# A hybrid decoder layer on one core: stored sums loaded behind the weights, and the order of sums at the seam of the MLP's matrices

## The chip, the cores and the metric

The kernel runs on one core of a Trainium2 chip. The time is the device time of one execution in microseconds (us). TensorE (PE) multiplies matrices, VectorE (DVE) and ScalarE (ACT) work on elements, GpSimd (POOL) and SyncE (SP) here mostly start transfers; the engines run side by side and wait for one another by semaphores.

## The reference, cut to what matters

512 rows of 2048 columns go through one layer: a norm, an input projection, a short gated convolution beside an attention, a merge through an output matrix with the residual, and then the MLP, where the change lies:

```
h = rmsnorm(x, g_mlp)
u = square(relu(einsum('bsd,df->bsf', h, w_ff1)))     # 2048 -> 8192
x = x + einsum('bsf,fd->bsd', u, w_ff2)               # 8192 -> 2048
return rmsnorm(x, g_final)
```

All of it is float32.

## The kernel before

Each large product is done with Strassen-Winograd's scheme: one level, seven products of half-size blocks in place of eight, named A11, A12, S4, S2, S3, S1, A22 after their left or right operands. The operands of S1 to S4 are sums of blocks. Each float32 operand is split into a high part of a type that TensorE takes (`th`, made by ACT in `high_of`, L111) and a low part, the rest (`tl`, made by DVE in `low_of`, L114); three multiplications (high by high, high by low, low by high) then make one product. So behind every weight block of 1 MB stand one ACT pass, one DVE pass and, for the S products, a DVE subtraction (`sub`, L128), and PE takes the high part first and the low part last. `th` and `tl` have two buffers each.

**First matrix.** `w_ff1` goes through in 16 groups of 512 columns (`Group`, `ff1`). From group 1 on a group is `head` (A11, A12) and `tail` (S4, S2, S3, S1, A22), with weights loaded by SP into four slots `x0` to `x3`. `put_u` scales and rectifies each quarter of the result, and `sums` squares it, forms the seven operands that the second matrix will want (a tile `r` of 7 blocks, by four short DVE operations in a row), splits them (ACT L1480 into `rh`, DVE L1481 back into `r`) and writes both to memory (`s_d`, L1483 and L1484, on POOL's queue). Sums that needn't be done at once are put off in the list `later` and done in the next group's `tail`, behind the copy `s2` of the accumulator `a` (`snap`, ACT L268) and ahead of product S3. That copy is also what frees bank `a` for product S1.

**Second matrix.** `w_ff2` goes through in 8 segments of 1024 rows, each in two units (`unit`) of 1024 columns, in the order A11, A12, S2, S3, S1, A22, S4. Its left operands are the stored sums: `load_sums` brings them in four pieces: piece 0 (A11, A12), piece 1 (S2, S3), piece 2 (S1, A22), piece 3 (S4), into tiles `us` that share their memory with operands of the first matrix. The weights `y00, y10, y01, y11` come by SP's queue into the same four slots, each as soon as its slot is free.

**The seam** is the first unit. Piece 0 is loaded on POOL's queue in the last group of `w_ff1`, piece 1 on POOL's queue behind that group, pieces 2 and 3 on SP's queue behind the first unit's weights. The first unit's subtractions are `y00 <- y01 - y00`, `t <- y11 - y00` (operand of S2), `y01 <- y11 - y01` (S3), `t <- y10 - t` (A22).

What sets the order: within one engine the framework places independent instructions by its own estimate of when they are ready, beginning from the order in the code; an instruction held by `keep_in_program_order` stays where the code has it, and `issue_after` puts what follows behind a given instruction. On the chip each engine takes its instructions strictly in the order given.

Of the kernel before, what the change touches and what calls it, by code (L numbers as in the profile page):

```python
# [8 lines left out]
F32 = mybir.dt.float32  # L9
# [36 lines left out]
def tile_hybrid_block(ctx: ExitStack, tc, x, g_mix, w_in, b_f, b_gate, conv_w, w_conv_out,  # L46
                      w_attn_out, w_mix_out, g_mlp, w_ff1, w_ff2, g_final, out):
    nc = tc.nc
    x, out = x[0], out[0]
# [35 lines left out]
    s_d = [dram.tile([P, 2, 4, 7, HS], F32, name=f"s_d{i}") for i in range(DFF // 1024)]  # L85
# [24 lines left out]
    def high_of(src, hi):  # L110
        return tied(nc.scalar.activation(out=hi, in_=src, func=AF.Copy))  # L111

    def low_of(src, hi, lo):
        return tied(nc.vector.tensor_tensor(out=lo, in0=src, in1=hi.bitcast(F32), op=ALU.subtract))  # L114

    def split(src, hi, lo):
        return high_of(src, hi), low_of(src, hi, lo)
# [9 lines left out]
    def sub(out, a, b):  # L127
        return nc.vector.tensor_tensor(out=out, in0=a, in1=b, op=ALU.subtract)  # L128

    def add(out, a, b):  # L130
        return nc.vector.tensor_tensor(out=out, in0=a, in1=b, op=ALU.add)
# [81 lines left out]
    free, later = [0, 1, 2, 3], []  # L213

    class Group:
# [3 lines left out]
        def __init__(self, view, c1, c2, w, ST, mm, banks, put, scale=1.0, extra={}, after=None, shift=SHIFT):  # L219
            self.extra, self.after, self.shift = extra, {} if after is None else after, shift  # L220
            self.view, self.cs, self.w, self.ST, self.mm, self.banks = view, (c1, c2), w, ST, mm, banks
            self.put, self.scale, self.at = put, scale, {}
            self.begun, self.queue, self.X = False, nc.sync, {}
            self.pinned, self.mid, self.apart, self.ready = False, {}, False, {}
            self.freed, self.summed, self.paced, self.half = lambda: None, False, False, {}
            self.nq = view.shape[0] // (2 * P)

        def load(self, i, j):
# [105 lines left out]
        def tail(self):  # L334

            X = self.quarters((0, 1), (1, 1))
            a = self.a
            c = self.acc("c")
            self.run(c, "S4", X[1, 1], True)
            sub(X[0, 0], X[0, 1], X[0, 0])  # L340
            sub(X[0, 1], X[1, 1], X[0, 1])
            sub(X[1, 1], X[1, 1], X[0, 0])
            self.run(a, "S2", X[1, 1], False)
            sub(X[1, 0], X[1, 0], X[1, 1])
            self.done(1, 1)
            s2 = self.snap(a)
            while later:
                later.pop(0)()
            d = self.acc("d")
            self.run(d, "S3", X[0, 1], True)  # L350
            self.done(0, 1)
            d1 = self.snap(d, self.scale)
            self.run(a, "S1", X[0, 0], False)
            self.done(0, 0)
            s4 = self.snap(a, self.scale)
            add(d1, d1, s4)
            self.put(1, 1, d1)
            self.plus(s4, c, self.scale)
            self.put(0, 1, s4)
            self.run(d, "A22", X[1, 0], False)  # L360
            self.done(1, 0)
            self.plus(s2, d)
            self.put(1, 0, s2)
# [384 lines left out]
    a, b = (gV0.acc(k)[0] for k in "ab")  # L748
# [771 lines left out]
    for g in range(4):  # L1520
# [24 lines left out]
        group = groups[g]  # L1545
# [55 lines left out]
    def load_sums(seg, ks, ST, queue=nc.gpsimd):  # L1601

        for k in ks:
            place, names = US[k]
            t = main.tile([P, 2, 4, len(names), HS], F32R, tag=f"t{place}", name="us")
            for e in range(2):
                queue.dma_start(out=t[:, e].bitcast(F32), in_=s_d[seg][:, e, :, 2 * k:2 * k + len(names)])
            for e, n in enumerate(names):
                ST[n] = moving(t[:, :, :, e])

    for g in range(1, DFF // S):
        group = ff1(g, ((2 + 2 * (g % 2),), (3,), (1 if g < DFF // S - 1 else 2,), (7,)))
        group.head(True, order=((0, 0), (0, 1), (1, 0)))
        if g == DFF // S - 1:
            us0 = {}
            load_sums(0, (0,), us0)
        group.tail()

    load_sums(0, (1,), us0)
    later.pop()()  # L1620
    ph.close()
    pp.close()
# [70 lines left out]
    def unit(seg, cg, ST):  # L1693

        a, d = banks2(cg, "a"), banks2(1 - cg, "d")
        if seg == 0:
            kept[cg] = banks2(2 + cg, "b")
        b = kept[cg]  # L1700
        X, at = {}, {}
        end = seg == NSEG - 1 and cg == 1
        for i, j in ((0, 1), (1, 1), (0, 0), (1, 0)) if end else ((0, 0), (1, 0), (0, 1), (1, 1)):
            at[i, j] = free.pop(0)
            t = main.tile([P, 4, S], F32, tag=f"x{at[i, j]}", name=f"y{i}{j}")
            c = NW * cg + S * j
            src = w_ff2[seg * 1024:(seg + 1) * 1024, c:c + S].rearrange("(q two p) c -> two p q c", two=2, p=P)
            nc.sync.dma_start(out=t, in_=src[i])
            X[i, j] = t

        def run(ps, n, src, first):
            hi, lo = parts([P, 4, S])
            split(src, hi, lo)
            mm_rows(ps, ST[n], hi, lo, first)

        last = seg == NSEG - 1
        begun = set()

        def into(i, j, ps, end=False):
            for e in range(2):  # L1720
                xs = place(i, j, cg, e)[2]
                if last and end:
                    finish(i, j, cg, ps, e)
                elif seg == 0 and (i, j) not in begun:
                    nc.scalar.activation(out=xs, in_=ps[e], func=AF.Copy)
                elif (i, j, cg) in in_rows:
                    onto_rows(i, j, cg, ps, e)
                else:
                    add(xs, ps[e], xs)
            begun.add((i, j))  # L1730

        t2 = main.tile([P, 4, S], F32, tag="t0", name="t2")
        if end:


            one = const.tile([P, 1], F32, name="one")
            nc.vector.tensor_copy(one, turned[:, 0:1])
            sub(t2, X[1, 1], X[0, 1])
            run(a, "A11", X[0, 0], True)
            onto_rows(0, 0, cg, a, 1)  # L1740
            onto_rows(0, 0, cg, a, 0, one)
            nc.vector.memset(one, 1.0)
            run(d, "S3", t2, True)
            sub(X[0, 0], X[0, 1], X[0, 0])
            sub(X[0, 1], X[1, 1], X[0, 0])
            into(1, 1, d)
            run(a, "S2", X[0, 1], False)
            sub(X[0, 1], X[1, 0], X[0, 1])
            into(1, 0, a)
            for t in (2, 3):  # L1750
                gain(t, one)
            run(d, "A22", X[0, 1], False)
            into(1, 0, d, True)
            run(a, "S1", X[0, 0], False)
            into(1, 1, a, True)
            p4 = (main.tile([P, 4, S], F32R, tag="t0", name="th4"),
                  main.tile([P, 4, S], F32R, tag=f"x{at[0, 1]}", name="tl4"))
            split(X[1, 1], *p4)
            for t in (2, 3):
                Final(t).all()  # L1760
            p2 = parts([P, 4, S])
            split(X[1, 0], *p2)
            for t in (0, 1):
                gain(t, one)
            for e in range(2):
                mm_rows(b, ST["A12"], *p2, False, blocks=(e,))
                finish(0, 0, cg, b, e)
                mm_rows(a, ST["S4"], *p4, False, blocks=(e,))
                finish(0, 1, cg, a, e)
                Final(e).all()  # L1770
            return
        run(a, "A11", X[0, 0], True)
        sub(X[0, 0], X[0, 1], X[0, 0])
        into(0, 0, a)
        run(b, "A12", X[1, 0], seg == 0)
        if seg == 0 and cg == 0:
            load_sums(0, (2, 3), us0, nc.sync)
        if last:
            into(0, 0, b, True)
        sub(t2, X[1, 1], X[0, 0])  # L1780
        run(a, "S2", t2, False)
        sub(X[0, 1], X[1, 1], X[0, 1])
        sub(t2, X[1, 0], t2)
        free.append(at[1, 0])
        into(1, 0, a)
        run(d, "S3", X[0, 1], True)
        free.append(at[0, 1])
        into(1, 1, d)
        run(a, "S1", X[0, 0], False)
        free.append(at[0, 0])  # L1790
        into(1, 1, a, True)
        run(d, "A22", t2, False)
        into(1, 0, d, True)
        run(a, "S4", X[1, 1], False)
        free.append(at[1, 1])
        into(0, 1, a, True)
        if 3 <= seg < 7:
            residual(*((0, 0), (1, 0), (1, 1), (0, 1))[seg - 3], cg)
# [42 lines left out]
```

## Time and profile before

| | |
|---|---|
| median of 3 runs | 2413.63 us (2411.69 to 2413.76) |
| the profiled execution | 2415.49 us, span 2413.4 us |
| PE busy | 2396.1 us of the span (99%) |
| DVE, ACT, POOL busy | 2029.7 us (84%), 1205.2 us (50%), 297.8 us (12%) |
| instructions | 41,364 |
| bytes moved by DMA | 491.98 MB |
| granted TensorE clock | 0.999 |

A row of a timeline is: start, length, engine, line, operation, what it writes and reads, count, and in brackets how long the engine had been idle before it and who released it. Where several equal instructions stand together the length is that of all. The lines L... are those of the kernel before. A matmul's length is modelled and overlaps the next one's; the distance between starts is the better measure of PE's pace. A row of a DMA view has KB each and the time from issue to landing.

### The profile page before, as it was taken

The numbers are of one execution on the slowest core, as the hardware profiler recorded it, in microseconds if no ns is written. First come the engines' busy times: TensorE is split into PE (matmuls) and PEld (weight loads), VectorE is DVE, ScalarE is ACT, GpSimd is POOL, SyncE is SP. The second block draws the span as 40 slices with busy tenths as digits, with TensorE's granted clock in tenths as the row PEclk, the third lists the DMA queues.
The fourth block names the chain that finished last, engine by engine and source line by source line (L and its number), as shares of the span: only waits on it lengthen the run. The fifth ranks groups of instructions, "written<-read, shape, count | busy, mean of one in ns | idle before, by whom it ended". The sixth has DMA issues, their size and how long they took to land. (4 is left out here: it accounts for less than half of the span.)

```text
span 2413.4 us, 41364 instructions
## 1 busy us (share of the span) xinstructions
PE 2396.1 (99%) x17778; PEld 2259.7 (94%) x17778; DVE 2029.7 (84%) x1683; ACT 1205.2 (50%) x1238; POOL 297.8 (12%) x476
## 2 busy tenths in 40 slices
PE   9999999999999999999999999999999999999998
PEld 9999999999999999899999999999998888888886
DVE  7987677789888778889988889888887888889898
ACT  7443444445555534456666666665664333333334
POOL 1110111121111112023300000000011001100000
PEclk9999999999999999999999999999999999999999
DMA  8664544564565756566856564655678567665662
GB/s 276 190 189 152 156 147 152 154 205 158 172 209 175 262 180 209 165 211 223 311 195 217 194 231 172 222 207 197 231 294 293 165 209 253 218 211 184 233 230 102
DMA packets 281127, 491.98 MB, mean 204 GB/s; under 512 B 11820, under 2 KB 192136, under 8 KB 280560
## 3 DMA queue, kind: packets, MB, share of 16 engines
q1 hardware_dynamic: 228496, 275.86, 36.1%
q0 software_dynamic: 51840, 212.42, 24.0%
q8 instruction: 139, 2.28, 0.4%
q10 hardware_dynamic: 608, 1.06, 0.1%
q14 instruction: 44, 0.36, 0.0%
HBM read 379.70 MB, written 109.07 MB: 203 GB/s over the span
## 5 line engine op out<-in xcount | busy, mean ns | idle before, releaser
L111 ACT ACTIVATE th<-x 128x2048 fp32r<-128x2048 f32 (+1 forms) x280 | 537.1, 1918 | 487.9 <-DVE x L128 165.4
L114 DVE TENSOR_TENSOR tl<-x,th 128x2048 fp32r<-128x2048 f32 (+2 forms) x282 | 639.7, 2274 | 156.2 <-ACT th L111 152.4
L128 DVE TENSOR_TENSOR x<-x,x 128x2048 f32<-128x2048 f32 (+1 forms) x160 | 366.1, 2288 | 22.0 <-DMA x<-in_w_in_dram 16.9
L111 ACT ACTIVATE th<-y 128x2048 fp32r<-128x2048 f32 (+1 forms) x109 | 185.3, 1701 | 272.1 <-PE a L197 138.8
L114 DVE TENSOR_TENSOR tl<-y,th 128x2048 fp32r<-128x2048 f32 (+1 forms) x109 | 219.0, 2014 | 28.3 <-ACT th L111 27.8
L195 PE MATMUL a<-th,us 128*128 128x512 f32 x512 | 199.3, 389 | 0.0
L197 PE MATMUL a<-th,us 128*128 128x512 f32 x512 | 199.2, 389 | 0.0
L171 PE MATMUL c<-S,th 128*128 128x256 f32 x848 | 196.0, 277 | 0.0
L175 PE MATMUL c<-S,th 128*128 128x256 f32 x848 | 195.8, 277 | 0.0
L171 PE MATMUL a<-S,th 128*128 128x256 f32 x784 | 182.4, 278 | 0.2 <-ACT o L268 0.2
L175 PE MATMUL a<-S,th 128*128 128x256 f32 x784 | 180.8, 276 | 0.0
L171 PEld LDWEIGHTS c<-S,th 128*128 128x128 f32 x848 | 159.3, 188 | 0.1
L175 PEld LDWEIGHTS c<-S,th 128*128 128x128 f32 x848 | 159.3, 188 | 0.0
L171 PEld LDWEIGHTS a<-S,th 128*128 128x128 f32 x784 | 147.3, 188 | 0.9 <-issue 0.5
L175 PEld LDWEIGHTS a<-S,th 128*128 128x128 f32 x784 | 147.3, 188 | 0.5 <-issue 0.5
L199 PE MATMUL a<-tl,us 128*128 128x512 f32 x512 | 136.9, 389 | 0.6 <-DVE tl L114 0.6
L171 PE MATMUL b<-A,th 128*128 128x256 f32 x544 | 126.2, 278 | 1.4 <-ACT th L111 1.4
L171 PE MATMUL a<-A,th 128*128 128x256 f32 x544 | 126.8, 279 | 0.0
L171 PE MATMUL d<-S,th 128*128 128x256 f32 x544 | 126.3, 278 | 0.0
L171 PE MATMUL d<-A,th 128*128 128x256 f32 x544 | 125.8, 277 | 0.0
L175 PE MATMUL a<-A,th 128*128 128x256 f32 x544 | 125.7, 277 | 0.0
L175 PE MATMUL b<-A,th 128*128 128x256 f32 x544 | 125.6, 277 | 0.0
(407 smaller groups left out, 6028.4 us busy)
## 6 DMA issues: line engine op xcount, KB each, us to landing
x<-in_w_in_dram SPq DMA_DIRECT2D x86, 1024.0 KB, 6.0
y<-in_w_ff_dram SPq DMA_DIRECT2D x64, 1024.0 KB, 7.7
x<-in_w_ff_dram SPq DMA_DIRECT2D x60, 1024.0 KB, 8.2
us<-s_d POOLq DMA_DIRECT2D x46, 1024.0 KB, 9.5
s_d<-rh POOLq DMA_DIRECT2D x32, 896.0 KB, 5.7
s_d<-r POOLq DMA_DIRECT2D x32, 896.0 KB, 6.1
x<-in_w_mix_out_dram SPq DMA_DIRECT2D x17, 1024.0 KB, 6.8
g_d<-o POOLq DMA_DIRECT2D x32, 256.0 KB, 3.1
```

The costliest lines, as they stand in the source:

```text
L111: return tied(nc.scalar.activation(out=hi, in_=src, func=AF.Copy))
L114: return tied(nc.vector.tensor_tensor(out=lo, in0=src, in1=hi.bitcast(F32), op=ALU.subtract))
L128: return nc.vector.tensor_tensor(out=out, in0=a, in1=b, op=ALU.subtract)
L171: i = nc.tensor.matmul(o, hi[:, q, js], Sh, start=first and q == 0 and j == 0, stop=False, skip_group_check=True)
L175: nc.tensor.matmul(o, hi[:, q, js], Sl, start=False, stop=False, skip_group_check=True)
L195: tied(nc.tensor.matmul(o, Sh, hi[:, q, :], start=begin and q == 0, stop=False, skip_group_check=True))
L197: tied(nc.tensor.matmul(o, Sl, hi[:, q, :], start=False, stop=False, skip_group_check=True))
L199: tied(nc.tensor.matmul(o, Sh, lo[:, q, :], start=False, stop=q == nq - 1, skip_group_check=True))
```

## The change

Three things are changed.

- Piece 1 of the stored sums is loaded by SP, behind the first unit's four weight blocks and ahead of pieces 2 and 3, no longer by POOL behind the last group; SP's loads of these pieces are held in program order.
- In the first unit, `t <- y10 - t` is done behind the low part of S3 (`tl<-y01`) and no longer ahead of it.
- In group 1 of the first matrix, the put-off sums stand in the code behind product S3 and the copy of its result, no longer ahead of S3.

```diff
@@ class Group
+            self.late = False
@@ tail
             s2 = self.snap(a)
-            while later:
+            while later and not self.late:
                 later.pop(0)()
             d = self.acc("d")
             self.run(d, "S3", X[0, 1], True)
             self.done(0, 1)
             d1 = self.snap(d, self.scale)
+            while later:
+                later.pop(0)()
             self.run(a, "S1", X[0, 0], False)
@@ load_sums
-                queue.dma_start(out=t[:, e].bitcast(F32), in_=s_d[seg][:, e, :, 2 * k:2 * k + len(names)])
+                i = queue.dma_start(out=t[:, e].bitcast(F32), in_=s_d[seg][:, e, :, 2 * k:2 * k + len(names)])
+                if queue is nc.sync:
+                    tc.keep_in_program_order(i)
@@ groups of w_ff1
         group.head(True, order=((0, 0), (0, 1), (1, 0)))
+        group.late = g == 1
...
-    load_sums(0, (1,), us0)
     later.pop()()
@@ unit
+        begins = seg == 0 and cg == 0
+        if begins:
+            load_sums(0, (1, 2, 3), us0, nc.sync)
...
         run(b, "A12", X[1, 0], seg == 0)
-        if seg == 0 and cg == 0:
-            load_sums(0, (2, 3), us0, nc.sync)
...
         sub(X[0, 1], X[1, 1], X[0, 1])
-        sub(t2, X[1, 0], t2)
+        if not begins:
+            sub(t2, X[1, 0], t2)
+        into(1, 0, a)
+        low = run(d, "S3", X[0, 1], True)
+        if begins:
+            with tc.issue_after(low.ins):
+                sub(t2, X[1, 0], t2)
         free.append(at[1, 0])
-        into(1, 0, a)
-        run(d, "S3", X[0, 1], True)
```

PE's order of instructions is the same as before, row for row. On the other engines it moves in three places (line numbers in the changed kernel are 1 to 12 higher; the numbers behind `x`, `y` and `t` count allocations).

ACT in group 1, from the copy of the held squares `r<-c` to the copy of bank `a`; `th<-x_13212` is the high part of S3's operand, `th<-x_13210` that of S1's. Before:

```order
L1469 ACTIVATE r<-c 128x512
L1464 ACTIVATE r<-o 128x256
L1464 ACTIVATE c<-o 128x512
L111 ACTIVATE th<-x_13212 128x2048
L1480 ACTIVATE rh<-r 128x1792
L111 ACTIVATE th<-x_13210 128x2048
L268 ACTIVATE o<-a 128x512
```

Now:

```order
L1472 ACTIVATE r<-c 128x512
L111 ACTIVATE th<-x_13212 128x2048
L1467 ACTIVATE r<-o 128x256
L1467 ACTIVATE c<-o 128x512
L1483 ACTIVATE rh<-r 128x1792
L111 ACTIVATE th<-x_13210 128x2048
L269 ACTIVATE o<-a 128x512
```

S3's high part has moved ahead of two copies of the sums; `rh`, S1's high part and the copy of bank `a` stand as before. DVE at the same place, from the low part of S2's operand (`tl<-x_13326`) to that of S1's. Before:

```order
L114 TENSOR_TENSOR tl<-x_13326,th 128x2048
L131 TENSOR_TENSOR r<-o,r 128x256
L128 TENSOR_TENSOR r<-r,o 128x256
L128 TENSOR_TENSOR r<-r 128x256
L114 TENSOR_TENSOR tl<-x_13212,th 128x2048
L128 TENSOR_TENSOR r<-r 128x256
L1481 TENSOR_TENSOR r<-r,rh 128x1792
L114 TENSOR_TENSOR tl<-x_13210,th 128x2048
```

Now:

```order
L114 TENSOR_TENSOR tl<-x_13326,th 128x2048
L114 TENSOR_TENSOR tl<-x_13212,th 128x2048
L131 TENSOR_TENSOR r<-o,r 128x256
L128 TENSOR_TENSOR r<-r,o 128x256
L128 TENSOR_TENSOR r<-r 128x256 x2
L1484 TENSOR_TENSOR r<-r,rh 128x1792
L114 TENSOR_TENSOR tl<-x_13210,th 128x2048
```

S3's low part stood between the third and the fourth of the short sums; now all four stand behind it. DVE in the first unit of the second matrix (`t` is S2's and then A22's operand, `y_19640`, now `y_19637`, is `y01`, `y_19636`, now `y_19633`, is `y00`). Before:

```order
L128 TENSOR_TENSOR t_19644<-y_19642,y_19636 128x2048
L128 TENSOR_TENSOR r<-r 128x256
L128 TENSOR_TENSOR y_19640<-y_19642,y_19640 128x2048
L114 TENSOR_TENSOR tl<-t_19644,th 128x2048
L1481 TENSOR_TENSOR r<-r,rh 128x1792
L128 TENSOR_TENSOR t_19644<-y_19638,t_19644 128x2048
L114 TENSOR_TENSOR tl<-y_19640,th 128x2048
```

Now:

```order
L128 TENSOR_TENSOR t_19650<-y_19639,y_19633 128x2048
L128 TENSOR_TENSOR r<-r 128x256
L128 TENSOR_TENSOR y_19637<-y_19639,y_19637 128x2048
L114 TENSOR_TENSOR tl<-t_19650,th 128x2048
L1484 TENSOR_TENSOR r<-r,rh 128x1792
L114 TENSOR_TENSOR tl<-y_19637,th 128x2048
L128 TENSOR_TENSOR t_19650<-y_19635,t_19650 128x2048
```

The last two rows have changed places. On the queues, POOL loses two loads of 1 MB that stood between the stored sums of the last group; SP gains them behind `y11` and ahead of pieces 2 and 3.

More of the change, by code (lines that the diff above doesn't have):

```diff
@@ L1709, in unit @@
             X[i, j] = t
+        begins = seg == 0 and cg == 0
+        if begins:
+            load_sums(0, (1, 2, 3), us0, nc.sync)
         def run(ps, n, src, first):
             hi, lo = parts([P, 4, S])
-            split(src, hi, lo)
+            low = split(src, hi, lo)[1]
             mm_rows(ps, ST[n], hi, lo, first)
+            return low
         last = seg == NSEG - 1
```

## The prediction

> **What bounds the kernel now.** First the page's busy times: PE is busy almost throughout, so an edit can win only where PE stands still or runs below its pace.
>
> ```profile
> PE 2396.1 (99%) x17778; PEld 2259.7 (94%) x17778; DVE 2029.7 (84%) x1683; ACT 1205.2 (50%) x1238; POOL 297.8 (12%) x476
> ```
>
> Next, PE's timeline at the seam: the first rows of A12, S2, S3 and S1, and the two low parts that came late.
>
> ```profile
> 1797.74 0.39 PE L195 MATMUL b<-th,us 128*128 128x512 f32 x1
> ...
> 1803.18 0.48 PE L195 MATMUL a<-th,us 128*128 128x512 f32 x1
> ...
> 1805.89 1.21 PE L199 MATMUL a<-tl,us 128*128 128x512 f32 x4 [0.62 <-DVE tl L114]
> ...
> 1809.70 0.39 PE L195 MATMUL d<-th,us 128*128 128x512 f32 x1
> ...
> 1812.23 1.20 PE L199 MATMUL d<-tl,us 128*128 128x512 f32 x4 [0.56 <-DVE tl L114]
> ...
> 1816.02 0.39 PE L195 MATMUL a<-th,us 128*128 128x512 f32 x1
> ```
>
> A12 takes 1803.18 - 1797.74 = 5.44 us. S2 takes 6.52 and S3 6.32: 1.08 and 0.88 too long, 1.96 us in all, both for a low part of DVE's. So the question is why DVE is late; its timeline, with two rows of ACT's:
>
> ```profile
> 1789.39 0.69 DVE L131 TENSOR_TENSOR o<-o 128x512 f32<-128x512 f32 x1
> 1792.20 2.29 DVE L128 TENSOR_TENSOR y<-y,y 128x2048 f32<-128x2048 f32 x1 [2.13 <-DMA y<-in_w_ff_dram]
> ...
> 1798.81 2.29 DVE L128 TENSOR_TENSOR t<-y,y 128x2048 f32<-128x2048 f32 x1
> ...
> 1803.55 2.29 DVE L114 TENSOR_TENSOR tl<-t,th 128x2048 fp32r<-128x2048 f32 x1
> ...
> 1807.69 2.29 DVE L128 TENSOR_TENSOR t<-y,t 128x2048 f32<-128x2048 f32 x1
> 1809.89 4.49 DVE L114 TENSOR_TENSOR tl<-y,th 128x2048 fp32r<-128x2048 f32 x2
> ```
>
> ```profile
> 1801.19 1.92 ACT L111 ACTIVATE th<-t 128x2048 fp32r<-128x2048 f32 x1 [3.09 <-DVE t L128]
> ...
> 1805.08 1.91 ACT L111 ACTIVATE th<-y 128x2048 fp32r<-128x2048 f32 x1
> ```
>
> DVE waits 2.13 us for a transfer and is busy without a gap from there. The transfer is weight block `y01`. The issues of `y01`, `y11`, piece 2's second half (with both of piece 3) on SP's queue, and of piece 1 on POOL's:
>
> ```profile
> 1778.62 0.37 SPq L1708 DMA_DIRECT2D y<-in_w_ff_dram  x1
> ...
> 1784.06 0.37 SPq L1708 DMA_DIRECT2D y<-in_w_ff_dram  x1
> ...
> 1787.57 6.83 SPq L1607 DMA_DIRECT2D us<-s_d  x3
> ```
>
> ```profile
> 1781.86 1.53 POOL L1607 DMA_DIRECT2D us<-s_d  x2 [0.48 <-PE d L177]
> ```
>
> Their times to landing (`y01`, piece 1, piece 2's second half), and the queues' bytes from 1785 to 1792 (q1 is SP's, q0 POOL's):
>
> ```profile
> y<-in_w_ff_dram SPq DMA_DIRECT2D x1, 1024.0 KB, 13.5
> ...
> us<-s_d POOLq DMA_DIRECT2D x2, 1024.0 KB, 14.3
> ...
> us<-s_d SPq DMA_DIRECT2D x1, 1024.0 KB, 16.4
> ...
> q0 software_dynamic: 405, 1.96, 69.6%
> q1 hardware_dynamic: 435, 0.86, 32.5%
> ```
>
> `y01` lands at 1778.62 + 13.5 = 1792.1, which is when DVE goes on. In the 7 us before, POOL's queue moved 1.96 MB and SP's 0.86 MB.
>
> **Edit 1, piece 1 behind the weights.** POOL loses its 2 x 1024 KB = 2.1 MB. What is left on q0 is one write of stored sums (896 KB, 0.92 MB). The 0.86 MB that `y01` still lacked at 1785 then take, at the 2.82 MB per 7 us = 0.40 MB/us of both queues, 2.1 us if they go first and 4.4 us if the whole write goes first: `y01` lands between 1787.1 and 1789.4. DVE is free at 1789.39 + 0.69 = 1790.1 and starts its subtraction there, 2.1 us earlier; with no gap behind it the rows up to S2's low part move by as much. That one ends at 1803.55 + 2.29 - 2.1 = 1803.7; PE asks for it eight matmuls of 0.227 us (2.72 us for twelve) behind 1803.18, at 1805.0. S2's high part, which waited for `t`, moves ahead too. The first 1.08 us go, with 1.3 us to spare.
>
> What could be late instead is piece 1 itself, for S2 at 1803.2. Piece 2's second half lands at 1787.57 + 16.4 = 1804.0; piece 1 now stands ahead of it and of its other half in the same queue, with no byte added, so it lands 2.1 MB / 0.40 = 5.2 us earlier, near 1798.8. Even beside piece 2 it would cost 0.8 us. On SP its two issues fall between `y11` (1784.06) and piece 2 (1787), whose tile isn't free earlier; POOL had nothing else queued. Cost nothing, cover 4.4 us.
>
> [...]
>
> **Edit 2, `t <- y10 - t` behind S3's low part.** In S3's way on DVE stood one subtraction, 1809.89 - 1807.69 = 2.2 us. With it and the 2.1 us of edit 1, S3's low part could start at 1805.6; its high part ends by 1805.08 + 1.91 = 1807.0 at the latest, so the low part ends by 1809.3, and PE, now at S3 from 1803.18 + 5.44 = 1808.6, asks at 1810.4. The other 0.88 us go; either edit alone would do for them. Behind it the displaced subtraction (A22, two products later) and S1's low part end by 1812.5, needed at 1815.9: covered by 3.4 us. The slot of `y10` comes free a little later than that of `y01`, so the next unit's `y10` is issued before its `y00`; the latter is wanted some 15 us later, nothing. Seam: -1.96 us, between -0.9 (edit 1 fails) and -1.96.
>
> **Edit 3, the put-off sums of group 1.** ACT and DVE there, and PE's row:
>
> ```profile
> 1233.95 0.63 ACT L1469 ACTIVATE r<-c 128x512 f32<-128x512 f32 x1 [0.89 <-DMA s_d<-r]
> 1234.49 0.40 ACT L1464 ACTIVATE r<-o 128x256 f32<-128x256 f32 x1
> ...
> 1235.32 1.90 ACT L111 ACTIVATE th<-x 128x2048 fp32r<-128x2048 f32 x1
> 1239.97 1.71 ACT L1480 ACTIVATE rh<-r 128x1792 fp32r<-128x1792 f32 x1 [2.74 <-issue]
> 1241.58 1.90 ACT L111 ACTIVATE th<-x 128x2048 fp32r<-128x2048 f32 x1
> 1243.38 0.57 ACT L268 ACTIVATE o<-a 128x512 f32<-128x512 f32 x1
> ```
>
> ```profile
> 1235.36 0.42 DVE L131 TENSOR_TENSOR r<-o,r 128x256 f32<-128x256 f32 x1
> 1235.69 0.42 DVE L128 TENSOR_TENSOR r<-r,o 128x256 f32<-128x256 f32 x1
> ...
> 1237.26 2.29 DVE L114 TENSOR_TENSOR tl<-x,th 128x2048 fp32r<-128x2048 f32 x1 [0.81 <-ACT th L111]
> 1239.47 0.42 DVE L128 TENSOR_TENSOR r<-r 128x256 f32<-128x256 f32 x1
> ```
>
> ```profile
> 1244.01 0.38 PE L171 MATMUL a<-S,th 128*128 128x256 f32 x1 [0.22 <-ACT o L268]
> ```
>
> S1 waits for the copy of bank `a`, which waits on ACT behind `rh` and S1's high part; `rh` waits for the fourth short sum, which sat behind S3's low part. The new order doesn't lift the copy over `rh`. S3's high part starts at 1234.49 and ends at 1236.39, its low part runs 1236.4 to 1238.6, and all four short sums follow at 0.33 us each: the last ends at 1240.1 where it ended at 1239.9. So `rh`, the copy and S1 come 0.2 us later: +0.2 us, not a gain (bounds: -0.4 if the stall went after all, +0.4 for twice the shift). S3's own low part had 2 us to spare and needs nothing.
>
> More hangs on that stall than its length. The chain, whose rows are the low parts of one product each, and one stretch of the windows (the number behind POOL's is the clock):
>
> ```profile
> 1248.05 1.88 PE a L177 x16
> ...
> 1310.34 1.88 PE c L177 x16
> ...
> 1321.43 1.81 PE d L177 x16
> 1326.87 1.81 PE a L177 x16
> ```
>
> ```profile
> 1240.00:1280.00 40.00, 39.78 (x339) 39.59 (x338) 35.03 (x26) 27.45 (x27) 2.13 (x4) 1.00 0.62 214
> ```
>
> From the stall to about 1312 the eleven steps between these rows take 62.29 / 11 = 5.66 us, later ones 5.44: 0.22 us a product, over twelve products 2.7 us, at a granted clock of 1.00. Something of how matmuls fall in step after the stall lasts until another disturbance ends it. A stall of another length may end in the fast step or in the slow one; the likeliest is that it stays slow.
>
> [...]
>
> **Sum.** -1.96 + 0.2 = -1.8 us: the profiled execution would go from 2415.49 to 2413.7 (span 2413.4 to 2411.6), the median from 2413.63 to **2411.9**. The profiled one lies 1.9 us above the median and the runs 2.1 us apart, as much as the gain.
>
> **Rivals.**
> - *The slow stretch goes* (32%). For it: in the later groups, with no stall, the step is 5.44; against it: the stall stays and grows. -1.96 - 2.7 + 0.2 = -4.5: 2409.2.
> - *Order buys no bytes* (12%). Piece 1's bytes stay, and if `y01` shared with them as before, it would land at 1792.1 again. S2's 1.08 us stay, edit 2 alone still wins 0.88: -0.9 + 0.2: 2412.9. Against it: on SP's queue piece 1 stands behind `y01`. [...]
> - *The slow stretch grows* (10%), on the other side. It ended in the second group behind the stall; each further group of seven products costs 7 x 0.22 = 1.5 us. With two more the gain is gone, with three it is -1.8 + 4.6 = +2.8: 2416.4. For it: the longer stall; against it: from 1320 on all is fast.
>
> **How the numbers follow.** The forecast has the other 46%. The range is 2408.0 to 2414.4: the forecast within the runs' spread, the third case, most of the second, the fourth up to two groups; about 18% lie outside. A measurement of this kernel can tell about 0.2%, 4.8 us, from no change. Faster by more (below 2408.8) is just under half of the second case, 0.14, and 0.02 of the rest: 0.16. Slower by more (above 2418.5) needs five more slow groups: 0.04. Within: 0.80.
>
> **What would show it.** At the seam: no idle of PE for a low part, S2 and S3 at 5.44 us each, DVE's first subtraction near 1790 without a wait, `y01` landed within 11 us, piece 1 within 15 us of its issue. In group 1: `rh` 0.2 us later against S3's first row, the wait of S1 for the copy still there at 0.3 to 0.5 us. The steps behind it, 5.66 or 5.44, decide between forecast and second case. It is wrong if PE waits for piece 1, or if a stretch of 5.66 lasts beyond 1320.

## The result, and the profile after

| | before | changed |
|---|---|---|
| median of 22 runs | 2413.93 us (2411.51 to 2420.04) | 2411.48 us (2409.0 to 2415.85) |
| ratio, 95% interval | | 0.9987 (0.9982 to 0.9993) |
| the profiled execution | 2415.49 us, span 2413.4 us | 2412.44 us, span 2410.7 us |

The ratio is a gain of 3.1 us, between 1.7 and 4.3 (the two medians lie 2.45 us apart): faster, and by less than the 0.2% (4.8 us) that the prediction gives as the bound of no change. Busy times of the changed kernel, from its profile page:

```profile
span 2410.7 us, 41365 instructions
...
PE 2394.6 (99%) x17778; PEld 2259.0 (94%) x17778; DVE 2029.7 (84%) x1683; ACT 1204.7 (50%) x1238; POOL 295.5 (12%) x474
```

At the seam, PE's timeline of the changed kernel, with the first rows of A11, A12, S2, S3 and S1:

```profile
1791.68 0.40 PE L195 MATMUL a<-th,us 128*128 128x512 f32 x1
...
1797.15 0.39 PE L195 MATMUL b<-th,us 128*128 128x512 f32 x1
...
1802.59 0.39 PE L195 MATMUL a<-th,us 128*128 128x512 f32 x1
...
1808.03 0.39 PE L195 MATMUL d<-th,us 128*128 128x512 f32 x1
...
1813.47 0.39 PE L195 MATMUL a<-th,us 128*128 128x512 f32 x1
```

S2 and S3 take 1808.03 - 1802.59 = 5.44 and 1813.47 - 1808.03 = 5.44 us, and no row of PE's there has a bracket, so PE was not idle. From A12 to S1 it is 16.32 us where it was 1816.02 - 1797.74 = 18.28: the 1.96 us are gone. DVE's timeline of the changed kernel at the same place:

```profile
1788.80 0.69 DVE L131 TENSOR_TENSOR o<-o 128x512 f32<-128x512 f32 x1
1790.35 2.29 DVE L128 TENSOR_TENSOR y<-y,y 128x2048 f32<-128x2048 f32 x1 [0.86 <-DMA y<-in_w_ff_dram]
...
1801.70 2.29 DVE L114 TENSOR_TENSOR tl<-t,th 128x2048 fp32r<-128x2048 f32 x1
...
1805.84 2.29 DVE L114 TENSOR_TENSOR tl<-y,th 128x2048 fp32r<-128x2048 f32 x1
1808.04 2.29 DVE L128 TENSOR_TENSOR t<-y,t 128x2048 f32<-128x2048 f32 x1
1810.24 2.29 DVE L114 TENSOR_TENSOR tl<-y,th 128x2048 fp32r<-128x2048 f32 x1
```

The wait for `y01` is shorter (0.86 us for 2.13) but not gone. S2's low part ends at 1803.99, and PE asks for it eight matmuls behind 1802.59, at 1804.41: 0.4 us to spare. S3's low part ends at 1808.13, wanted near 1809.9. The displaced subtraction (1808.04) and S1's low part follow, in time. The issue of `y01` on SP's queue in the changed kernel (with that of `y11`), and its DMA view: packets, MB and share of each queue from 1785 to 1790.2 us, when `y01` landed, and the time to landing of `y10`, the load issued ahead of `y01`, and of `y01`:

```profile
1778.02 5.81 SPq L1713 DMA_DIRECT2D y<-in_w_ff_dram  x2
```

```profile
q1 hardware_dynamic: 591, 1.17, 62.0%
q0 software_dynamic: 136, 0.86, 40.1%
...
y<-in_w_ff_dram SPq DMA_DIRECT2D x1, 1024.0 KB, 11.1
...
y<-in_w_ff_dram SPq DMA_DIRECT2D x1, 1024.0 KB, 12.2
```

The same view of the kernel before, `y10`:

```profile
y<-in_w_ff_dram SPq DMA_DIRECT2D x1, 1024.0 KB, 8.7
```

`y01`, issued at 1778.02, landed 12.2 us later, at 1790.2, and the load ahead of it was 2.4 us slower than before. Piece 1, issued behind `y11` from 1784.05 on, landed 11.6 us (first half) and 13.3 us later; PE never waited for it.

In group 1, ACT's timeline and PE's row of S1, in the changed kernel:

```profile
1233.05 0.63 ACT L1472 ACTIVATE r<-c 128x512 f32<-128x512 f32 x1 [0.76 <-DMA s_d<-r]
1233.59 1.91 ACT L111 ACTIVATE th<-x 128x2048 fp32r<-128x2048 f32 x1
...
1239.37 1.71 ACT L1483 ACTIVATE rh<-r 128x1792 fp32r<-128x1792 f32 x1 [3.05 <-issue]
1240.99 1.90 ACT L111 ACTIVATE th<-x 128x2048 fp32r<-128x2048 f32 x1
1242.79 0.57 ACT L269 ACTIVATE o<-a 128x512 f32<-128x512 f32 x1
```

```profile
1243.42 0.38 PE L171 MATMUL a<-S,th 128*128 128x256 f32 x1 [0.39 <-ACT o L269]
```

S1 still waits for the copy of bank `a`, 0.39 us instead of 0.22. And the slow stretch behind it is still there; the chain of the changed kernel:

```profile
1247.45 1.89 PE a L177 x16
...
1309.75 1.88 PE c L177 x16
...
1320.83 1.81 PE d L177 x16
1326.27 1.81 PE a L177 x16
```

(1309.75 - 1247.45) / 11 = 5.66 us a product, then 5.44, as before. The account of the two executions: seam -1.96, stall of group 1 +0.2, and -0.8 that was there ahead of group 1's S2, where the change has not acted yet; together -2.6 of the -2.7 us between the spans.

### The profile page after: what moved, and what is told of

The parts are those of the page before. It is cut to its first block, busy times and chain, and to the rows that moved or that the text cites. A ratio compares the mean times of both kernels' runs of the same rounds, so it can differ in the third digit from the quotient of the medians.

```text
span 2410.7 us, 41365 instructions
## 1 busy us (share of the span) xinstructions
PE 2394.6 (99%) x17778; PEld 2259.0 (94%) x17778; DVE 2029.7 (84%) x1683; ACT 1204.7 (50%) x1238; POOL 295.5 (12%) x474
## 4 chain that ended last, share of the span: by engine, by line
PE 89%; DVE 4%; issue 2%; DMA 2%; ACT 2%; POOL 0%; SPq 0%; DVEq 0%; POOLq 0%; ACTq 0%
PE a L171 6%; PE a L177 6%; PE a L175 6%; PE d L171 5%; PE d L175 5%; PE d L177 5%; PE a L199 5%; PE a L197 5%; PE a L195 5%; PE c L171 4%; PE c L177 4%; PE c L175 4%; PE d L195 3%; PE d L197 3%; PE d L199 3%; PE b L171 3%
```

## The experiments

Ten executions, one trace each, bear on it. The table gives for each what was lost at the seam (from the first row of A11 to the first of S1, less 4 x 5.44 = 21.76 us), the time of `y01` from issue to landing, DVE's wait for it, S1's stall in group 1 (PE's idle time ahead of its first row), and the products at the slow step (5.65 us in place of 5.44) behind it; all in us but the products. The rows that carry the verdicts follow with each experiment. The edits are shortened, with `...` where code is left out.

| kernel | lost at the seam | `y01` | DVE's wait | stall in group 1 | slow products behind it | span |
|---|---|---|---|---|---|---|
| before | 1.98 | 13.5 | 2.13 | 0.22 | 12 | 2413.4 |
| changed | 0.03 | 12.2 | 0.86 | 0.39 | 12 | 2410.7 |
| e1, edit 1 alone | 0.67 | 12.2 | 0.83 | none | 7, from the spare matmul on | 2412.2 |
| e2, edit 2 alone | 3.72 | 16.1 | 4.78 | none | 0 | 2413.8 |
| e3, edit 3 alone | 3.78 | 15.3 | 3.92 | 0.47 | 12 | 2415.4 |
| e4, changed, sums later still | 0.02 | 12.4 | 1.00 | none | 0 | 2408.7 |
| e5, before, second trace | 4.40 | 15.9 | 4.54 | 0.50 | 0 | 2416.4 |
| e6, changed without edit 3 | 0.12 | 12.6 | 1.19 | 0.20 | 0 | 2410.9 |
| e7, changed, second trace | 0.02 | 11.2 | none | none | 0 | 2408.6 |
| e8, changed, no spare matmul | 0.03 | 12.3 | 0.49 | none | 95, from the second group's S2 on | 2427.7 |

The stretch ahead of group 1, which no edit touches, differs between executions too: S1 of group 1 starts at 1243.4 to 1244.3 in six of them, but at 1245.3 to 1247.15 in e2, e1, e6 and e5. In e2 PE ran at the slow step there already, from 1189 to the spare matmul of group 1 at 1234. So single spans are not compared, only stretches.

**e1: edit 1 alone.**

```diff
+    load_sums(0, (1, 2, 3), us0, nc.sync)      # first unit, behind its weight blocks, in program order
-    load_sums(0, (1,), us0)                    # POOL, behind the last group
-    load_sums(0, (2, 3), us0, nc.sync)         # first unit, behind A12
```

> The kernel before with edit 1 alone (piece 1 of the stored sums on SP's queue behind the four weight blocks). My theory, that DVE is late at the seam because y01 shares the DMA engines with piece 1: y01 lands 8.5 to 11 us after its issue (13.5 before), DVE's first subtraction starts without a wait, S2 and S3 take 5.44 us each (6.52 and 6.32 before), both stalls gone though edit 2 is missing; S3's low part is ready only 0.4 us ahead of need. Rival, that the order of queues buys no bytes: y01 lands near 13.5 us, S2 stays near 6.5. Second rival, that piece 1 is late: PE stands at S2's high part, for a DMA.

DVE's first subtraction and the seam's only stall, from the timeline of e1:

```profile
1791.08 2.29 DVE L128 TENSOR_TENSOR y<-y,y 128x2048 f32<-128x2048 f32 x1 [0.83 <-DMA y<-in_w_ff_dram]
...
1811.12 1.20 PE L199 MATMUL d<-tl,us 128*128 128x512 f32 x4 [0.35 <-DVE tl L114]
```

S2 is clean, S3 is not: 0.67 us are lost. So edit 1 was not enough for S3 here, against the forecast. By the forecast's rows S3's low part would end at 1809.89 - 2.1 + 2.2 = 1810.0 for a PE that asks at 1810.4; with `y01` 0.83 us late these 0.4 us are gone.

**e2: edit 2 alone**, the subtraction behind S3's low part.

```diff
-        sub(t2, X[1, 0], t2)
+        begins = ...                           # the first unit
+        if not begins: sub(t2, X[1, 0], t2)
         into(1, 0, a)
-        run(d, "S3", X[0, 1], True)
+        low = run(d, "S3", X[0, 1], True)
+        if begins:
+            with tc.issue_after(low.ins): sub(t2, X[1, 0], t2)
```

> The kernel before with edit 2 alone (t <- y10 - t behind S3's low part). My theory: y01 still lands near 13.5 us, S2 stays at 6.5 us, S3 falls to 5.44 (its low part 2.2 us earlier, 0.88 us were missing): the seam from S2's first row to S1's first row takes 11.96 us (12.84 before, 10.88 with all edits). Rival, that S3's stall was only S2's lateness passed on: S3 stays at 6.3.

PE's timeline of e2, the rows with a wait, and DVE's that starts it:

```profile
1799.56 1.20 PE L199 MATMUL b<-tl,us 128*128 128x512 f32 x4 [1.22 <-DVE tl L114]
...
1804.44 0.50 PE L195 MATMUL a<-th,us 128*128 128x512 f32 x1 [0.94 <-ACT th L111]
...
1807.17 1.20 PE L199 MATMUL a<-tl,us 128*128 128x512 f32 x4 [0.63 <-DVE tl L114]
```

```profile
1793.48 2.29 DVE L128 TENSOR_TENSOR y<-y,y 128x2048 f32<-128x2048 f32 x1 [4.78 <-DMA y<-in_w_ff_dram]
```

S3 is clean: behind its first row there is no wait. But DVE waited 4.78 us, more than twice what the forecast's trace had, and with that A12 and S2's high part stall too. From S2's first row to S1's it is 11.94 us, as expected; the loss lies mostly ahead of it. Lost in all: 3.72 us. The question that this put was which wait is usual with POOL's load in place.

**e3: edit 3 alone.**

```diff
-            while later:
+            while later and not self.late:
                 later.pop(0)()
             d = self.acc("d")
             self.run(d, "S3", X[0, 1], True)
...
             d1 = self.snap(d, self.scale)
+            while later:
+                later.pop(0)()
...
+        group.late = g == 1
```

> The kernel before with edit 3 alone (put-off sums of group 1 behind S3). My theory: the copy of bank a comes later against PE by 0.2 us, PE idles 0.4 us ahead of S1 (0.22 before), about twelve products at 5.66 us follow, the seam stays at 12.84 us: +0.2 us. Rival, that the edit takes the stall away: no idle ahead of S1, 5.44 us a product from there, -3 us.

PE's row of S1 in group 1, from the timeline of e3:

```profile
1244.09 0.38 PE L171 MATMUL a<-S,th 128*128 128x256 f32 x1 [0.47 <-ACT o L269]
```

The stall is longer than in the first trace of before, and the slow stretch is there. At the seam, whose code is that of before, 3.78 us were lost with `y01` 15.3 us behind its issue: a second execution with the seam of before that lost about twice the 1.96.

**e5: the kernel before, traced again**, since e2 and e3 left open what before usually loses.

> The kernel before once more, for a second trace of it. Theory A, that its seam varies with the landing of y01: y01 lands later than in the first trace (13.5 us), at 15 to 16 us as with edit 2 or edit 3 alone, and from A11's to S1's first row PE loses 3.5 to 4 us against 4 x 5.44 (1.98 in the first trace). Theory B, that edits 2 and 3 moved y01: 13.5 us and about 2.0 us lost, as in the first trace. In group 1: a stall of 0 to 0.4 us ahead of S1, the step fast or slow.

The timeline of e5, PE's waits with the first rows of A11 and S1, and DVE's wait:

```profile
1247.15 0.39 PE L171 MATMUL a<-S,th 128*128 128x256 f32 x1 [0.50 <-ACT o L268]
...
1792.86 0.40 PE L195 MATMUL a<-th,us 128*128 128x512 f32 x1
...
1801.27 1.20 PE L199 MATMUL b<-tl,us 128*128 128x512 f32 x4 [0.97 <-DVE tl L114]
...
1806.15 0.50 PE L195 MATMUL a<-th,us 128*128 128x512 f32 x1 [0.96 <-ACT th L111]
...
1819.02 0.39 PE L195 MATMUL a<-th,us 128*128 128x512 f32 x1
```

```profile
1795.19 2.29 DVE L128 TENSOR_TENSOR y<-y,y 128x2048 f32<-128x2048 f32 x1 [4.54 <-DMA y<-in_w_ff_dram]
```

With the same code as in the forecast's trace, `y01` landed 15.9 us behind its issue instead of 13.5, and 1819.02 - 1792.86 - 21.76 = 4.40 us were lost at the seam, more than the 3.5 to 4 expected. Three executions with the seam of before lost 1.98, 3.78 and 4.40 us; the forecast was made from the one that lost least. The first row says more: behind a stall of 0.50 us PE went on at the fast step.

**e4: the put-off sums behind the copy of bank `a`**, which lifts the copy over `rh`, as edit 3 does not.

```diff
             if len(ps) == 1:
-                nc.scalar.activation(out=s, ...)
+                self.copied = nc.scalar.activation(out=s, ...)
...
             s2 = self.snap(a)
+            copied = self.copied
...
             while later:
-                later.pop(0)()
+                with tc.issue_after(copied.ins):
+                    later.pop(0)()
             self.run(a, "S1", X[0, 0], False)
```

> The changed kernel, but in group 1 the put-off sums are issued behind the copy of bank a that frees it for S1. Theory 1, that the slow stretch is a child of the stall: no idle of PE ahead of S1, 5.44 us a product all the way through groups 1 to 3, 0.55 + 12 x 0.22 = 3.2 us less than the changed kernel, a ratio to the kernel before near 0.9975 (changed kernel 0.9987). [...]

The copy and what stands around it on ACT, and the chain, both of e4:

```profile
1236.96 1.93 ACT L111 ACTIVATE th<-x 128x2048 fp32r<-128x2048 f32 x1 [1.70 <-PE a L175]
1238.79 0.59 ACT L269 ACTIVATE o<-a 128x512 f32<-128x512 f32 x1
1239.27 0.62 ACT L1474 ACTIVATE r<-c 128x512 f32<-128x512 f32 x1
...
1242.75 1.71 ACT L1485 ACTIVATE rh<-r 128x1792 fp32r<-128x1792 f32 x1 [1.73 <-issue]
```

```profile
1247.80 1.81 PE a L177 x16
...
1307.75 1.81 PE c L177 x16
```

The copy is about 5 us earlier against PE (0.2 us behind S3's first row, 1238.57, where the changed kernel has 5.4), the stall is gone, and the step is (1307.75 - 1247.80) / 11 = 5.45 us. The median of 11 runs is 2410.92 us, ratio 0.9984 (0.9975 to 0.9993) against a before of 2414.9 us. The trace is as theory 1 expected; its ratio of 0.9975 lies at the very edge of the interval, and within the intervals this is no more than the changed kernel has.

**e6: the changed kernel without edit 3.**

```diff
-        group.late = g == 1
```

> The changed kernel without edit 3 (edits 1 and 2 alone). My theory: the seam is clean (no idle of PE, 21.8 us from A11's to S1's first row); S1 of group 1 stalls by 0 to 0.4 us in place of 0.4 to 0.5, so the time is the changed kernel's or up to 1 us less, ratio to the kernel before 0.998 to 0.9987. Rival, that edit 3 earns part of the gain: ratio above 0.9992, 1 us or more behind the changed kernel.

**e7: the changed kernel again**, on the chip of e5, e6 and e8.

> The changed kernel once more, on the chip of the others: ratio to the kernel before near 0.9987 as in the first comparison; in its second trace a clean seam, y01 landing within 12 to 12.5 us of its issue, a stall of 0.4 to 0.5 us ahead of S1 in group 1 and 5.66 us a product behind it.

e6: 2410.90 us, ratio 0.9983 (0.9974 to 0.9992). e7: 2410.59 us, ratio 0.9986 (0.9977 to 0.9995). The intervals lie on each other: edit 3 is worth nothing that these runs can measure. Of e7's trace only the clean seam came as expected; `y01` landed sooner (11.2 us), S1 of group 1 had no stall, and the fast step followed. S1's row in group 1 of e6, and DVE's first subtraction in e7:

```profile
1246.02 0.39 PE L171 MATMUL a<-S,th 128*128 128x256 f32 x1 [0.20 <-ACT o L269]
```

```profile
1787.23 2.29 DVE L128 TENSOR_TENSOR y<-y,y 128x2048 f32<-128x2048 f32 x1
```

Both went on at the fast step behind group 1's S1, e6 with a stall. In e7 DVE did not wait for `y01` at all; of the five executions with edits 1 and 2 only this one shows that.

**e8: the changed kernel without the spare matmul** (192 columns, one a group, ahead of the first row of product S2, not the fifth as the expectation says; nothing reads its result) in groups 1 to 15. It was to tell whether the pace of PE is a state that lasts until something disturbs it, or the price of the stall.

```diff
-                     extra={"A12": "first", "S3": "first"} if g == 0 else apart(0, "S2", 0))
+                     extra={"A12": "first", "S3": "first"} if g == 0 else {})
```

> The changed kernel without the spare matmul of 192 columns that stands ahead of the fifth weight row of product S2 in groups 1 to 15 (its result is used by nothing). Theory 1, that PE's step is drawn anew at each disturbance and lasts until the next: the stall of group 1 draws 5.66 us, nothing draws again, and it lasts to the end of the first matrix: 85 more products x 0.22, +19 us, near 2430. Theory 2, that the stretch ends by itself or by what the other engines do: it ends near 1312 as before, and the time is that of the changed kernel less about 15 x 0.1 us.

The time was 2429.4 us, the span 2427.7: 17.0 us more than the changed kernel's. PE's timeline and chain of e8, where the pace turns and where it ends (the last row of the timeline is the second matrix's first):

```profile
1271.50 0.36 PE L171 MATMUL a<-S,th 128*128 128x256 f32 x1
1271.70 0.28 PE L175 MATMUL a<-S,th 128*128 128x256 f32 x1
...
1808.65 0.40 PE L195 MATMUL a<-th,us 128*128 128x512 f32 x1
```

```profile
1778.66 1.89 PE b L177 x16
1784.31 1.88 PE c L177 x16
...
1806.92 1.89 PE d L177 x16
```

It was not the stall of group 1 that began it, as theory 1 had it: S1 of group 1 has none here, and the fast step goes on. In the next group two starts lie 0.20 us apart in place of 0.11, with no wait named, and from there PE runs at 5.65 us a product to the end of the first matrix, 1808.65 - 1271.50 = 537 us: 95 products x 0.21 = 20.0 us, less the 2.6 us that the changed kernel's own stretch cost, less the spare matmuls themselves (15, at 0.09 us each), is about 16 of the 17.0. So in this trace the pace is a state that nothing ended until the second matrix began, and with the spare matmuls in place it never lasted that long: each such stretch of the first matrix in the other traces ends at one. A spare matmul doesn't always set the fast step: in e1 the slow stretch begins at one and ends at the next, and in before, the changed kernel and e3 it takes two. Such a hitch doesn't always set the slow step either: in e7 the first two starts of group 1's S1 lie 0.21 us apart, in e8 itself those of group 1's S2 0.22, and the fast step follows.

## Why the prediction was right or wrong

**The time and the range.** 2411.9 us were forecast, 2411.48 measured; faster, as the likeliest case said, by less than 0.2%. The gain forecast was 1.8 us, the measured one 3.1, so part of the nearness is luck: the seam's term was too small, as follows.

**Seam: mechanism right, term mis-sized.** "-1.96 between -0.9 and -1.96": the two stalls and their cause stand. All five traces with edits 1 and 2 (changed, e4, e6, e7, e8) lose 0.02 to 0.12 us there, and all three with the seam of before (before, e3, e5) 1.98 to 4.40. What failed is the taking of one execution's loss for the loss: the other two lost 3.78 and 4.40, so that the three have a mean of 3.4, beside a measured gain of 3.1 (1.7 to 4.3). The end of -1.96 was the end for that one execution only. That this execution lay 1.9 us above the median was no sign of a large loss at the seam, since executions differ by as much ahead of group 1 (S1 of group 1 starts at 1247.15 in e5, at 1244.01 in the trace of the forecast).

**`y01`'s landing: out of its bounds.** Forecast "between 1787.1 and 1789.4", which is 8.5 to 10.8 us behind its issue, and DVE without a wait. It landed 12.2 us behind its issue (12.2 to 12.6 in five traces with edit 1, 11.2 in e7), 1.4 us later than the later bound. The step that failed is the 0.86 MB that `y01` "still lacked at 1785": that is what SP's queue moved from 1785 to 1792, and not `y01` alone. SP's queue from the issue of `y00` on, in before from 1772.39 to 1785:

```profile
q1 hardware_dynamic: 1301, 2.60, 58.4%
```

In the changed kernel from 1771.8 to 1785, and to 1790.25, when `y01` landed:

```profile
q1 hardware_dynamic: 1425, 2.85, 58.9%
...
q1 hardware_dynamic: 2025, 4.03, 59.9%
```

The blocks `y00`, `y10` and `y01` have 3.15 MB together. So at 1785 `y01` lacked about 0.55 MB in before and 0.30 in the changed kernel, if nothing of `y11` had moved yet, and when it landed there, 0.88 MB of later loads had moved too. So bytes over rate didn't give the landing here. The traces keep sixteen landing signals for each load, which is over with the last. From issue to the fifteenth and to the sixteenth, in us:

| kernel | `y10` | `y01` |
|---|---|---|
| before | 8.2, 8.7 | 12.8, 13.5 |
| e5, before | 8.1, 11.3 | 13.1, 15.9 |
| e2, edit 2 alone | 9.0, 11.7 | 13.8, 16.1 |
| e3, edit 3 alone | 7.9, 11.0 | 13.1, 15.3 |
| changed | 8.3, 11.1 | 12.0, 12.2 |
| e1, edit 1 alone | 8.0, 11.0 | 11.8, 12.2 |
| e7, changed | 8.2, 9.7 | 11.0, 11.2 |

The last signal lags: that of `y10` is 1.4 to 3.2 us behind the fifteenth in the nine other traces (e4, e6 and e8 included) and 0.5 in the trace of the forecast, and with POOL's load in place that of `y01` follows 2.2 to 2.8 us late in e2, e3 and e5 and 0.7 in the forecast's. In the changed kernel fourteen signals of `y01` had come 10.9 us behind its issue, at the later bound, and the last two made it 12.2. This cost S2's cover, 0.4 us instead of the 1.3 us forecast, though nothing of the time. The small lag in the forecast's trace is also most of the reason why it lost least at the seam.

**"Either edit alone would do for" S3: wrong.** e1 loses 0.67 us on S3 with edit 1 alone; edit 2 alone keeps S3 clean (e2), while A12 and S2 lose 3.72. The two are worth more together: edit 1 brings `y01` 1 to 5 us nearer (13.5, 15.3, 15.9 and 16.1 against 11.2 to 12.6), and edit 2 gives the slack for the last 0.8. By these single traces most of the seam's gain is edit 1's.

**Piece 1: right.** It landed at 1798.4 where 1798.8 was forecast, within 13.3 us of its issue, and PE never waited for it.

**Edit 3: right in size, too small to show in the times.** "+0.2, not a gain": S1 stalled 0.39 us for 0.22, in e3 0.47. But its stall differs as much between executions of one code, because the copy `r<-c` on ACT, ahead of `rh`, waits for a DMA that lands at various times: this wait was 0.89 us in before and 1.19 in e5, and the stall 0.22 and 0.50; it was 0.76 in the changed kernel and 0.19 in e7, and the stall 0.39 and none. e6 against e7 shows no price.

**The slow stretch: stayed, as forecast, in the trace of the changed kernel, and that is partly luck.** "A stall of another length may end in the fast step or in the slow one" holds, and so the first rival (2409.2, the stretch goes) is not another outcome but another draw of the same kernel: e7 is the changed kernel without the stretch, at 2410.3 us and a span of 2408.6. "More hangs on that stall than its length" holds in part: in e5 and e6 the fast step follows the stall, and in e1, e2 and e8 a slow stretch begins elsewhere, in e1 and e8 without a stall. "How matmuls fall in step" is shown by no run. What is shown is the price: at a granted clock of 0.999 the slow step, 4% longer (5.65 us a product in place of 5.44), cost e8 some 16 us.

**The other rivals.** "Order buys no bytes": fallen, since `y01` takes 13.5 to 16.1 us in the four traces with POOL's load and 11.2 to 12.6 in the six without. "The slow stretch grows" past 1320: not in any trace with the spare matmuls; e8 shows what it costs without them.

**Open.** What decides between the fast and the slow step behind a hitch: neither the length of the stall (0.22 slow, 0.20 and 0.50 fast) nor its presence does. Why the last of a load's sixteen signals lags, and did so little in the forecast's trace. And whether edit 1 helps by the place in SP's queue or only because piece 1 is loaded later: it was not tried later on POOL's queue. e4 and e6 are, within their intervals, as fast as the changed kernel; none of the three is shown to be the best.

## What to carry to other kernels

Look for a load in another queue that runs beside the one the path waits for and is needed later: here, moved behind it in the same queue, it cost PE nothing and `y01` landed some 3 us sooner on the mean (15.2 us in four traces, 12.1 in six). A stall that hangs on a transfer should be sized from several executions, since one trace gave about half of what two others lost. And the bytes that a queue moves in a stretch are not those of one load: here the load that the path waited for was over 1.4 us behind its bound, with its last two signals.

## What was not expected of the hardware

PE ran at two paces at the same granted clock of 0.999: 113.3 and 117.7 ns between 256-column matmuls (5.44 and 5.65 us a product). In e8 the slower one began without any wait, where two starts lay 0.20 us apart, and it then lasted 537 us; in the traces with the spare matmuls it ended at one of these, behind 7 products in e1 and 12 in before, the changed kernel and e3. The landing of one and the same load, behind the same instructions, varied by 2.4 us between two executions of before, from 13.5 to 15.9 us, 2.1 of it between the last two of sixteen signals, and what it cost at the seam from 1.98 to 4.40.
